# Two Strassen-Winograd x steps and the end of a feed-forward: the order of products, of column halves and of additions to x

## The chip, the cores and the metric

The kernel runs on one core of one Trainium2 chip. The core has TensorE (PE in the profile; its weight loads are PEld), VectorE (DVE), ScalarE (ACT), GpSimd (POOL, unused here but for setting up) and SyncE (SP), whose queue issues the transfers from memory. Each engine works through its own queue in order; semaphores join them. Matmul results go to PSUM, eight banks of 128 x 512 float32. The metric is the time of one launch on the device in microseconds (us).

## The reference

A two-layer encoder over 256 tokens with 2048 columns, all in float32.

```python
x = x + neighbourhood_attention(rms_norm(x, na_norm), ...)       # layer 0
x = x + sq_relu_mlp(rms_norm(x, ffn0_norm), ffn0_w1, ffn0_w2)
x = x + dilated_attention(rms_norm(x, dil_norm), ...)            # layer 1
x = x + sq_relu_mlp(rms_norm(x, ffn1_norm), ffn1_w1, ffn1_w2)
return rms_norm(x, final_norm)

def sq_relu_mlp(h, w1, w2):                                      # w1: 2048 x 8192, w2: 8192 x 2048
    return jnp.square(jax.nn.relu(h @ w1)) @ w2
```

## The kernel before

**Precision.** Every float32 operand is split into a high part rounded to the matmul's own format (wh, xT, hT: ScalarE, line 190) and the rest (wl: VectorE, line 191). A product is three matmuls: high x high, high x low, low x high (lines 195 to 197).

**Steps.** The whole kernel is one list of steps, and the loop at the end of the file runs them in turn. A step is one weight tile of 128 x 4 x 512 and has four quarters of matmuls. Around them the loop puts other work, in this order: the quarter's matmuls, the transposes and small matmuls asked for at that quarter, `after[n]` (functions that follow quarter n), `prep(i + 2, n)` (casting the weights of the step two further on), and what has to be done with the transposes. After the four quarters come `evac`, the rest of the casting (`prep(i + 2, 3)`), `load(i + 5)` (the transfers of the step five further on, on SP's queue) and `post`. So the order of each engine's queue is written out by hand.

**A feed-forward** (`ffn`) goes four times through: two gemms of w1 (each 1024 of the 2048 hidden columns of that quarter), squared relu, transposes of the result to hT, and two gemms of w2 (each 1024 columns of x, into which the result is added). 

**A gemm** (`gemm_pair`) is eight steps, one for each pair of 128-row blocks of the inner dimension. Six of them, kind "s", multiply 2 x 2 blocks in the usual way: 8 products, 24 matmuls, into the four banks "2" (rows 0, columns 0), "3" (rows 0, columns 1), "4" (rows 1, columns 0) and "S" (rows 1, columns 1). Two, kind "x" (pairs 3 and 5), use seven products of sums of blocks: 21 matmuls, and four further banks "1", "5", "6", "7". The sums on the weights' side are made by VectorE and split again: sums (line 136), hs (ScalarE, line 176), ls (line 133); part of `prep_x`. The table X gives the seven in order, two to a quarter, with the number of the weight part that each takes: 2 and 3 are cast with the step's first half, 4 to 7 are the sums, 1 is cast last.

After the last x step `begin` puts banks "1", "6", "7", "5" together into a tile C of four quarters (rows x columns), one operation behind each quarter of the step that follows. After each quarter of the gemm's last step `end` adds the bank of that quarter. For w1, squared relu then works on C. For w2, `residual` adds C to x, 1024 columns at a time, when the step is over (`rows`).

**Banks.** `sum_banks` gives a gemm its eight banks and lets two neighbours swap halves: the banks "1", "6", "7", "5" of a gemm are the "2", "4", "S", "3" of the one before. Until a gemm's first x step they are spare, in the order "1", "6", "7", "5", and transposes take them (`ps.misc`): the four transposed groups of w1's second gemm, for instance, during the second and third step of the w2 gemm that follows; VectorE's last read of such a bank is hT, line 191.

**The ends of the two feed-forwards.** At the end of a feed-forward each 512 columns of x get their squares summed (`squares`), are transposed (`transposes`, line 384) and scaled into xT (`parts`, lines 407, 410, 412). Behind the first feed-forward stands the dilated attention's first gemm (`gemm_cols`, lines 220 and 222), of kind "a". There the third and fourth 512 columns are transposed in the attention's first and second step, then 1 / rms is spread by matmuls (`rows`, line 427, `cols`, line 441). Behind the second feed-forward stands the final norm; there alone the last gemm goes by `split_end`: the last two steps finish the left 512 columns first and then the right ones, both steps' weights being read in turn.

```python
for n in range(4):
    s.quarters(s, n)
    ...
    elif i and n < 3:
        prep(i + 2, n)
    ...
for f in s.evac:
    f()
...
prep(i + 2, 3)
load(i + 5)
for f in s.post:
    f()
```

Of the kernel before, what the change touches and what calls it, by code (L numbers as in the profile page):

```python
# [14 lines left out]
P = 128  # L15
T = 256
D = 2048
# [30 lines left out]
def tile_encoder(ctx: ExitStack, tc: tile.TileContext, ins, out):  # L48
# [217 lines left out]
    def sum_banks():  # L266

        if ps.order is None:
            l = ps.pair
            a, b = (l + 1) % 3, (l + 2) % 3  # L270
            ps.order = [2 * a, 2 * a + 1, 2 * b, 2 * b + 1, 6, 7, 2 * l, 2 * l + 1]
        order, ps.order = ps.order, ps.order[4:] + ps.order[:4]
        ps.spare = order[4:]
        return {q: order[n] for n, q in enumerate(("2", "4", "S", "3", "1", "6", "7", "5"))}

    STD = {(0, 0): "2", (0, 1): "3", (1, 0): "4", (1, 1): "S"}

    def gemm_pair(w, cp, A, sums_of, order, finish, split_end=False):
# [13 lines left out]
        def product(bank, a, b, last):  # L292
            if not q:
# [4 lines left out]
        X = (("1", "A11", 2), ("2", "A12", 3), ("6", "S2", 6), ("7", "S3", 4), ("5", "S1", 5), ("4", "A22", 7),  # L298
             ("3", "S4", 1))

        for n, (kind, pair) in enumerate(order):
# [7 lines left out]
            else:  # L309
                def quarter(s, m, pair=pair, n=n):  # L310
                    tb, c = ((0, 0), (1, 0), (1, 1), (0, 1))[m]
# [21 lines left out]
        def begin(m):  # L333
            if m == 0:
                C = q["C"] = part.pool.tile([P, 4, 512], F32, name="C", tag="C")
                nc.scalar.copy(C[:, 0, :], q["1"])
                q["U"] = scratch([P, 512], "U")
                subtract(nc.vector, q["U"], q["6"], C[:, 0, :])
            elif m == 1:
                subtract(nc.vector, q["C"][:, 2, :], q["U"], q["7"])  # L340
            elif m == 2:
                add(nc.vector, q["C"][:, 1, :], q["U"], q["5"])
            else:
                add(nc.vector, q["C"][:, 3, :], q["C"][:, 2, :], q["5"])

        def end(m):
            C = q["C"]
            if m == 0:
                add(nc.vector, C[:, 0, :], C[:, 0, :], q["2"])
            elif m == 1:  # L350
                subtract(nc.vector, C[:, 2, :], q["4"], C[:, 2, :])
            elif m == 2:
                add(nc.vector, C[:, 3, :], C[:, 3, :], q["S"])
            else:
                add(nc.vector, C[:, 1, :], C[:, 1, :], q["3"])

        s = made[first_x[-1] + 1]
        for m in range(4):
            s.after[m].append(lambda m=m: begin(m))
            if not split_end:  # L360
                made[-1].after[m].append(lambda m=m: end(m))
        finish(made, q)
        return made

# [300 lines left out]
    FF_LAST = [FF_ORDER[k] for k in (0, 1, 3, 2, 5, 4, 6, 7)]  # L665
# [6 lines left out]
    def ffn(norm, w1, w2, next_norm, next_done):  # L672
        for g in range(4):
            hT, sums = [None] * 4, {}

            def hidden(made, q, cp, hT=hT, sums=sums):
# [7 lines left out]
                for m, (tb, n) in enumerate(((0, 0), (1, 0), (1, 1), (0, 1))):  # L684
# [33 lines left out]
            def residual(made, q, cp):  # L718
                if last and next_norm() in fin and cp == 1:
                    def early():  # L720
                        add(nc.vector, x[:, 0, D // 2:], x[:, 0, D // 2:], both(q, 0))
                        subtract(nc.vector, x[:, 1, D // 2:D - 512], x[:, 1, D // 2:D - 512], q["C"][:, 2, :])
                        add(nc.vector, x[:, 1, D - 512:], x[:, 1, D - 512:], q["C"][:, 3, :])
                    made[-3].evac.append(early)
                    for tb in range(2):
                        made[-2].evac.append(lambda tb=tb: add(
                            nc.vector, x[:, tb, D // 2:D - 512], x[:, tb, D // 2:D - 512], q[STD[tb, 0]]))
                    made[-2].post.append(lambda: fin[0].squares(NB - 2))
                    made[-1].after[1].append(lambda: fin[0].finish(0, q["3"]))
                    made[-1].after[3].append(lambda: fin[0].finish(1, q["S"]))  # L730
                    return

                def rows(tb):
                    to = x[:, tb, cp * 1024:(cp + 1) * 1024]
                    add(nc.vector, to, to, both(q, tb))
                made[-1].evac.append(lambda: rows(1))
                made[-1].evac.append(lambda: rows(0))
                if last:
                    for c in (2 * cp, 2 * cp + 1):
                        made[-1].post.append(lambda c=c: next_norm().squares(c))  # L740
                        if next_done is not None:
                            next_done(made[-1], c, c % 2)

            def both(q, tb):
                return q["C"][:, 2 * tb:2 * tb + 2, :].rearrange("p a n -> p (a n)")

            for cp in range(2):
                end = last and next_norm() in fin and cp == 1
                gemm_pair(w2g, cp, hT, sums, FF_LAST if end else FF_ORDER,
                          lambda made, q, cp=cp: residual(made, q, cp), split_end=end)  # L750
# [161 lines left out]
    class Final:  # L912
# [32 lines left out]
        def finish(self, tb, acc):  # L945
            cs = slice((NB - 1) * 512, D)
            nc.vector.tensor_tensor(out=x[:, tb, cs], in0=x[:, tb, cs], in1=acc, op=ALU.add)
# [66 lines left out]
    for i, s in enumerate(steps):  # L1014
# [31 lines left out]
        if i < len(steps) - 2:  # L1046
            s.w = s.hi = s.lo = s.hs = s.sums = s.pair = None
# [66 lines left out]
```

## Time and profile before

| | |
|---|---|
| median of 3 runs | 2309.98 us (2309.74 to 2311.31) |
| the profiled execution | 2308.4 us, span 2306.6 us, mean granted clock 0.998 |
| PE busy | 2273.0 us, 99% of the span |
| DVE busy | 1758.8 us, 76% |
| ACT busy | 1217.7 us, 53% |
| DMA | 430.33 MB, mean 187 GB/s |

The span runs from the first to the last instruction; the time has what lies around it too. A matmul's end is modelled, so that two in a row overlap in the rows, and "busy" for PE is not PE at its peak. A line of the timeline gives start, duration, engine, line of the kernel, what is written from what, shapes, count, and in brackets how long the engine stood idle before and who ended that. A line of the waits gives engine and line that waited, who ended the wait, then us in total, times and the longest.

### The profile page before, as it was taken

The numbers are of one execution on the slowest core, as the hardware profiler recorded it, in microseconds if no ns is written. First come the engines' busy times: TensorE is split into PE (matmuls) and PEld (weight loads), VectorE is DVE, ScalarE is ACT, GpSimd is POOL, SyncE is SP. The second block draws the span as 40 slices with busy tenths as digits, with TensorE's granted clock in tenths as the row PEclk, the third lists the DMA queues.
The fourth block names the chain that finished last, engine by engine and source line by source line (L and its number), as shares of the span: only waits on it lengthen the run. The fifth ranks groups of instructions, "written<-read, shape, count | busy, mean of one in ns | idle before, by whom it ended". The sixth has DMA issues, their size and how long they took to land.

```text
span 2306.6 us, 28352 instructions
## 1 busy us (share of the span) xinstructions
PE 2273.0 (99%) x10988; PEld 1898.0 (82%) x10988; DVE 1758.8 (76%) x2082; ACT 1217.7 (53%) x1526; POOL 0.7 (0%) x6
## 2 busy tenths in 40 slices
PE   9999999999999999999999999999999999999998
PEld 7888888888888888887788888888888888888886
DVE  6666766788788788788877667757888788788787
ACT  6444545564564564565444544456554654554554
POOL 0000000000000000000000000000000000000000
PEclk9999999999999999999999999999999999999999
DMA  7555655656656656655554555555666566566563
GB/s 250 173 175 174 193 185 167 191 181 210 186 182 206 194 177 208 200 167 180 178 198 167 184 171 181 175 172 161 184 209 187 183 205 196 182 201 201 182 219 128
DMA packets 110727, 430.33 MB, mean 187 GB/s; under 512 B 23872, under 2 KB 24448, under 8 KB 92160
## 3 DMA queue, kind: packets, MB, share of 16 engines
q1 hardware_dynamic: 109920, 426.82, 57.4%
q8 instruction: 86, 1.41, 0.2%
q10 hardware_dynamic: 672, 1.70, 0.2%
q14 instruction: 49, 0.40, 0.0%
HBM read 426.38 MB, written 2.10 MB: 186 GB/s over the span
## 4 chain that ended last, share of the span: by engine, by line
PE 87%; DVE 5%; ACT 5%; issue 2%; DMA 1%; SPq 0%; ACTq 0%; DVEq 0%
PE banks L195 22%; PE banks L196 22%; PE banks L197 22%; PE banks L220 13%; PE banks L222 6%; ACT wh L190 2%; DVE wl L191 1%; DVE sums L136 1%; DVE ls L133 1%; ACT C L681 1%; ACT hs L176 1%; PE banks L694 1%; PE banks L384 1%; ACT C L682 0%; DMA bias<-in_rpb_dram 0%
## 5 line engine op out<-in xcount | busy, mean ns | idle before, releaser
L191 DVE TENSOR_TENSOR wl<-w,wh 128x1024 fp32r<-128x1024 f32 (+1 forms) x802 | 931.5, 1176 | 389.5 <-ACT wh L190 385.7
L190 ACT CAST wh<-w 128x1024 fp32r<-128x1024 f32 (+1 forms) x802 | 804.6, 1014 | 691.6 <-PE banks L197 478.4
L220 PE MATMUL banks<-xT,wh 128*128 128x512 f32 x1280 | 455.6, 399 | 0.5 <-ACT wh L190 0.4
L195 PE MATMUL banks<-wh,xT 128*128 128x512 f32 x1152 | 453.7, 394 | 0.0
L197 PE MATMUL banks<-wh,xT 128*128 128x512 f32 x1152 | 449.3, 390 | 0.0
L196 PE MATMUL banks<-wl,xT 128*128 128x512 f32 x1152 | 448.6, 389 | 0.6 <-DVE wl L191 0.6
L222 PE MATMUL banks<-xT,wl 128*128 128x256 f32 x1280 | 358.5, 280 | 2.3 <-DVE wl L191 2.3
L195 PE MATMUL banks<-wh,hT 128*128 128x512 f32 x832 | 327.2, 393 | 0.0
L197 PE MATMUL banks<-wh,hT 128*128 128x512 f32 x832 | 324.4, 390 | 0.0
L196 PE MATMUL banks<-wl,hT 128*128 128x512 f32 x832 | 323.8, 389 | 0.0
L220 PEld LDWEIGHTS banks<-xT,wh 128*128 128x128 f32 x1280 | 241.6, 189 | 55.6 <-ACT wh L190 1.5
L197 PEld LDWEIGHTS banks<-wh,xT 128*128 128x128 f32 x1152 | 216.2, 188 | 45.8
L196 PEld LDWEIGHTS banks<-wl,xT 128*128 128x128 f32 x1152 | 216.5, 188 | 43.9 <-DVE wl L191 0.9
L195 PEld LDWEIGHTS banks<-wh,xT 128*128 128x128 f32 x1152 | 216.5, 188 | 42.7
L222 PEld LDWEIGHTS banks<-xT,wl 128*128 128x128 f32 x1280 | 242.4, 189 | 3.7 <-DVE wl L191 3.4
L176 ACT CAST hs<-sums 128x2048 fp32r<-128x2048 f32 x64 | 122.5, 1914 | 156.5 <-DVE sums L136 156.5
L197 PEld LDWEIGHTS banks<-wh,hT 128*128 128x128 f32 x832 | 156.2, 188 | 33.0
L196 PEld LDWEIGHTS banks<-wl,hT 128*128 128x128 f32 x832 | 156.4, 188 | 31.8
L195 PEld LDWEIGHTS banks<-wh,hT 128*128 128x128 f32 x832 | 156.3, 188 | 31.3
L133 DVE TENSOR_TENSOR ls<-sums,hs 128x2048 fp32r<-128x2048 f32 x64 | 146.7, 2292 | 43.6 <-ACT hs L176 43.6
L136 DVE TENSOR_TENSOR sums<-sums,w 128x512 f32<-128x512 f32 x128 | 88.6, 692 | 4.4
L136 DVE TENSOR_TENSOR C<-C,banks 128x512 f32<-128x512 f32 x125 | 82.5, 681 | 0.0
(190 smaller groups left out, 2137.7 us busy)
## 6 DMA issues: line engine op xcount, KB each, us to landing
w<-in_ffn_w_dram SPq DMA_DIRECT2D x512, 512.0 KB, 5.0
w<-in_dil_wqkv_dram SPq DMA_DIRECT2D x72, 1024.0 KB, 4.9
w<-in_na_wqkv_dram SPq DMA_DIRECT2D x47, 1024.0 KB, 5.2
w<-in_na_wo_dram SPq DMA_DIRECT2D x16, 1024.0 KB, 4.9
w<-in_dil_wo_dram SPq DMA_DIRECT2D x8, 1024.0 KB, 4.8
bias<-in_rpb_dram SPq DMA_DIRECT2D x32, 96.0 KB, 8.6
out_dram<-x SPq DMA_DIRECT2D x8, 256.0 KB, 2.5
x<-in_x_dram SPq DMA_DIRECT2D x3, 512.0 KB, 9.0
```

The lines of the kernel that those rows point to most:

```text
L133: engine.tensor_tensor(out=out, in0=a, in1=b, op=ALU.subtract)
L136: engine.tensor_tensor(out=out, in0=a, in1=b, op=ALU.add)
L176: nc.scalar.copy(s.hs, s.sums)
L190: nc.scalar.copy(dst_hi, src)
L191: nc.vector.tensor_tensor(out=dst_lo, in0=src, in1=dst_hi.bitcast(F32), op=ALU.subtract)
L195: nc.tensor.matmul(o, left[0], right[0], start=start, stop=False)
L196: nc.tensor.matmul(o, left[0], right[1], start=False, stop=False)
L197: nc.tensor.matmul(o, left[1], right[0], start=False, stop=stop)
L220: nc.tensor.matmul(o, s.hi[a][:, cs], xt.rearrange("p h t -> p (h t)"), start=first, stop=False)
L222: nc.tensor.matmul(o[:, :T], s.lo[a][:, cs], xt[:, 0, :], start=False, stop=last)
L384: nc.tensor.transpose(self.tp[:, a, tb * P:(tb + 1) * P], x[:, tb, kt * P:(kt + 1) * P], ident)
L681: nc.scalar.activation(c, c, AF.Relu, scale=norm.r[:, tb:tb + 1])
```

## The change

- In the table X, product "5" moves from fifth to last of the seven; "4" and "3" move up.
- `begin` no longer has a tile U: 6 - 1 goes straight into C's second quarter, and bank "5" is added to two quarters of C by one operation of 1024 columns that reads the bank twice. It has three parts in place of four.
- `end` goes. For w1 the last addition to C stands in `last_sum`, at the same place. For w2 C is added to x during the last step (`early`), and each finished bank is added straight to x behind its quarter (`put`), 512 columns at a time.
- The last gemm of the first feed-forward too ends by column halves (`split_end`), with pairs 3 and 4 in changed places, so that its x steps are the fifth and sixth. Its third 512 columns of x are finished a step earlier, are transposed in its last step, in banks "2" and "4", and the fourth in the attention's first step.
- The tiles of a step are let go a step later.

```diff
@@ -271,8 +271,10 @@
             ps.order = [2 * a, 2 * a + 1, 2 * b, 2 * b + 1, 6, 7, 2 * l, 2 * l + 1]
         order, ps.order = ps.order, ps.order[4:] + ps.order[:4]
         ps.spare = order[4:]
-        return {q: order[n] for n, q in enumerate(("2", "4", "S", "3", "1", "6", "7", "5"))}
-
+        ps.taken = {q: order[n] for n, q in enumerate(("2", "4", "S", "3", "1", "6", "7", "5"))}
+        return ps.taken
+
+    QUARTERS = (0, 0), (1, 0), (1, 1), (0, 1)
     STD = {(0, 0): "2", (0, 1): "3", (1, 0): "4", (1, 1): "S"}
 
     def gemm_pair(w, cp, A, sums_of, order, finish, split_end=False):
@@ -295,8 +297,8 @@
             three(q[bank], a, b, bank not in touched, last)
             touched.add(bank)
 
-        X = (("1", "A11", 2), ("2", "A12", 3), ("6", "S2", 6), ("7", "S3", 4), ("5", "S1", 5), ("4", "A22", 7),
-             ("3", "S4", 1))
+        X = (("1", "A11", 2), ("2", "A12", 3), ("6", "S2", 6), ("7", "S3", 4), ("4", "A22", 7), ("3", "S4", 1),
+             ("5", "S1", 5))
 
         for n, (kind, pair) in enumerate(order):
             k, u = pair // 2, pair % 2
@@ -308,7 +310,7 @@
                         product(bank, left(pair, a), (s.hi[b], s.lo[b]), n == first_x[-1] and bank in "1567")
             else:
                 def quarter(s, m, pair=pair, n=n):
-                    tb, c = ((0, 0), (1, 0), (1, 1), (0, 1))[m]
+                    tb, c = QUARTERS[m]
                     for kk in range(2):
                         b = 2 * (1 - c) + kk
                         a = (("A11", "A12"), ("A21", "A22"))[tb][kk]
@@ -334,33 +336,25 @@
             if m == 0:
                 C = q["C"] = part.pool.tile([P, 4, 512], F32, name="C", tag="C")
                 nc.scalar.copy(C[:, 0, :], q["1"])
-                q["U"] = scratch([P, 512], "U")
-                subtract(nc.vector, q["U"], q["6"], C[:, 0, :])
+                subtract(nc.vector, C[:, 1, :], q["6"], C[:, 0, :])
             elif m == 1:
-                subtract(nc.vector, q["C"][:, 2, :], q["U"], q["7"])
+                subtract(nc.vector, q["C"][:, 2, :], q["C"][:, 1, :], q["7"])
             elif m == 2:
-                add(nc.vector, q["C"][:, 1, :], q["U"], q["5"])
-            else:
-                add(nc.vector, q["C"][:, 3, :], q["C"][:, 2, :], q["5"])
-
-        def end(m):
-            C = q["C"]
-            if m == 0:
-                add(nc.vector, C[:, 0, :], C[:, 0, :], q["2"])
-            elif m == 1:
-                subtract(nc.vector, C[:, 2, :], q["4"], C[:, 2, :])
-            elif m == 2:
-                add(nc.vector, C[:, 3, :], C[:, 3, :], q["S"])
-            else:
-                add(nc.vector, C[:, 1, :], C[:, 1, :], q["3"])
+                add(nc.vector, q["C"][:, 1::2, :], q["C"][:, 1:3, :], q["5"].unsqueeze(1).to_broadcast([P, 2, 512]))
 
         s = made[first_x[-1] + 1]
-        for m in range(4):
-            s.after[m].append(lambda m=m: begin(m))
-            if not split_end:
-                made[-1].after[m].append(lambda m=m: end(m))
+        for m in range(3):
+            s.after[0 if s is made[-1] else m].append(lambda m=m: begin(m))
         finish(made, q)
         return made
+
+    def last_sum(q, tb, c, out):
+
+        C, own = q["C"][:, 2 * tb + c, :], q[STD[tb, c]]
+        if (tb, c) == (1, 0):
+            subtract(nc.vector, out, own, C)
+        else:
+            add(nc.vector, out, C, own)
 
 
     class Norm:
@@ -662,7 +656,6 @@
 
     FF_PAIRS = (3, 5)
     FF_ORDER = [("x" if k in FF_PAIRS else "s", k) for k in range(8)]
-    FF_LAST = [FF_ORDER[k] for k in (0, 1, 3, 2, 5, 4, 6, 7)]
 
     parts = {len(steps) + 9: "feed-forward"}
     out_rows(ins["na_wo"], na_oT, 4, lambda: norms[1], begin_norm(1, False, FF_PAIRS),
@@ -681,7 +674,8 @@
                     nc.scalar.activation(c, c, AF.Relu, scale=norm.r[:, tb:tb + 1])
                     nc.scalar.activation(c, c, AF.Square)
 
-                for m, (tb, n) in enumerate(((0, 0), (1, 0), (1, 1), (0, 1))):
+                for m, (tb, n) in enumerate(QUARTERS):
+                    made[-1].after[m].append(lambda tb=tb, n=n: last_sum(q, tb, n, q["C"][:, 2 * tb + n, :]))
                     at_after(i, m, lambda tb=tb, n=n: squared_relu(tb, n))
                 for r in range(4):
                     held = {}
@@ -715,39 +709,56 @@
             w2g = w2[4 * g:4 * (g + 1)]
             last = g == 3
 
-            def residual(made, q, cp):
-                if last and next_norm() in fin and cp == 1:
-                    def early():
-                        add(nc.vector, x[:, 0, D // 2:], x[:, 0, D // 2:], both(q, 0))
-                        subtract(nc.vector, x[:, 1, D // 2:D - 512], x[:, 1, D // 2:D - 512], q["C"][:, 2, :])
-                        add(nc.vector, x[:, 1, D - 512:], x[:, 1, D - 512:], q["C"][:, 3, :])
-                    made[-3].evac.append(early)
+            def to(cp, tb, c):
+                return x[:, tb, cp * 1024 + c * 512:cp * 1024 + (c + 1) * 512]
+
+            def residual(made, q, cp, parted):
+                def put(tb, c):
+                    add(nc.vector, to(cp, tb, c), to(cp, tb, c), q[STD[tb, c]])
+
+                def early(n):
+                    C = q["C"]
+                    if n == 0:
+                        o = x[:, 0, cp * 1024:(cp + 1) * 1024]
+                        add(nc.vector, o, o, C[:, 0:2, :].rearrange("p a n -> p (a n)"))
+                    else:
+                        subtract(nc.vector, to(cp, 1, 0), to(cp, 1, 0), C[:, 2, :])
+                        add(nc.vector, to(cp, 1, 1), to(cp, 1, 1), C[:, 3, :])
+
+                if not parted:
+                    for n in range(2):
+                        made[-1].after[n].append(lambda n=n: early(n))
+                    for m, (tb, c) in enumerate(QUARTERS):
+                        made[-1].after[m].append(lambda tb=tb, c=c: put(tb, c))
+                    if last:
+                        for c in (2 * cp, 2 * cp + 1):
+                            made[-1].post.append(lambda c=c: next_norm().squares(c))
+                            if next_done is not None:
+                                next_done(made[-1], c, c % 2)
+                    return
+                for n in range(2):
+                    made[-2 if next_done is not None else -3].evac.append(lambda n=n: early(n))
+                for tb in range(2):
+                    made[-2].after[1 + 2 * tb].append(lambda tb=tb: put(tb, 0))
+                made[-2].post.append(lambda: next_norm().squares(NB - 2))
+                if next_norm() in fin:
                     for tb in range(2):
-                        made[-2].evac.append(lambda tb=tb: add(
-                            nc.vector, x[:, tb, D // 2:D - 512], x[:, tb, D // 2:D - 512], q[STD[tb, 0]]))
-                    made[-2].post.append(lambda: fin[0].squares(NB - 2))
-                    made[-1].after[1].append(lambda: fin[0].finish(0, q["3"]))
-                    made[-1].after[3].append(lambda: fin[0].finish(1, q["S"]))
+                        made[-1].after[1 + 2 * tb].append(lambda tb=tb: fin[0].finish(tb, lambda: put(tb, 1)))
                     return
-
-                def rows(tb):
-                    to = x[:, tb, cp * 1024:(cp + 1) * 1024]
-                    add(nc.vector, to, to, both(q, tb))
-                made[-1].evac.append(lambda: rows(1))
-                made[-1].evac.append(lambda: rows(0))
-                if last:
-                    for c in (2 * cp, 2 * cp + 1):
-                        made[-1].post.append(lambda c=c: next_norm().squares(c))
-                        if next_done is not None:
-                            next_done(made[-1], c, c % 2)
-
-            def both(q, tb):
-                return q["C"][:, 2 * tb:2 * tb + 2, :].rearrange("p a n -> p (a n)")
+                for tb in range(2):
+                    made[-1].after[1 + 2 * tb].append(lambda tb=tb: put(tb, 1))
+                made[-1].post.append(lambda: next_norm().squares(NB - 1))
+                made[-2].post.append(lambda: ps.spare.extend([ps.taken["2"], ps.taken["4"]]))
+                next_done(made[-2], NB - 2)
+                next_done(made[-1], NB - 1)
 
             for cp in range(2):
-                end = last and next_norm() in fin and cp == 1
-                gemm_pair(w2g, cp, hT, sums, FF_LAST if end else FF_ORDER,
-                          lambda made, q, cp=cp: residual(made, q, cp), split_end=end)
+                parted = last and cp == 1
+                order = FF_ORDER
+                if parted:
+                    order = [FF_ORDER[k] for k in ((0, 1, 2, 4, 3, 5, 6, 7), (0, 1, 3, 2, 5, 4, 6, 7))[next_done is None]]
+                gemm_pair(w2g, cp, hT, sums, order, lambda made, q, cp=cp, parted=parted: residual(made, q, cp, parted),
+                          parted)
 
     ffn(norms[1], ins["ffn0_w1"], ins["ffn0_w2"], lambda: norms[2], begin_norm(2, True))
 
@@ -942,9 +953,8 @@
                 nc.vector.tensor_scalar(out=self.part, in0=self.part, scalar1=1.0 / D, scalar2=EPS,
                                         op0=ALU.mult, op1=ALU.add)
 
-        def finish(self, tb, acc):
-            cs = slice((NB - 1) * 512, D)
-            nc.vector.tensor_tensor(out=x[:, tb, cs], in0=x[:, tb, cs], in1=acc, op=ALU.add)
+        def finish(self, tb, put):
+            put()
             self.square(NB - 1, tb)
             ms = small.tile([P, 1], F32, name="fms", tag="fms", bufs=2)
             nc.vector.tensor_scalar(out=ms, in0=self.ss[:, tb, NB - 1:], scalar1=1.0 / D,
@@ -1043,8 +1053,9 @@
         for f in s.post:
             f()
         run_late()
-        if i < len(steps) - 2:
-            s.w = s.hi = s.lo = s.hs = s.sums = s.pair = None
+        if i:
+            p = steps[i - 1]
+            p.w = p.hi = p.lo = p.hs = p.sums = None
     part.end()
 
 
```

## The prediction

> **What bounds the kernel now.** I read the profile's page first, then TensorE's waits (us in total, times, longest), then the page's DMA issues (KB, us to landing).
>
> ```profile
> span 2306.6 us, 28352 instructions
> PE 2273.0 (99%) x10988; PEld 1898.0 (82%) x10988; DVE 1758.8 (76%) x2082; ACT 1217.7 (53%) x1526; POOL 0.7 (0%) x6
> ...
> PE banks L195 <- DVE hT L191: 6.9, 8, 0.9
> PE banks L196 <- DVE ls L133: 3.3, 3, 1.4
> PE banks L384 <- DVE x L136: 0.8, 2, 0.4
> ...
> w<-in_ffn_w_dram SPq DMA_DIRECT2D x512, 512.0 KB, 5.0
> ```
>
> TensorE is busy for 2273.0 of 2306.6 us, so only the waits can be won: at most 33.6 us, and here the largest item is one wait that comes eight times. The timeline shows it at the first of the eight (start, duration, instruction, idle before).
>
> ```profile
> 513.16 0.40 PE L196 MATMUL banks<-ls,hs 128*128 128x512 f32 x1
> 513.39 0.40 PE L197 MATMUL banks<-hs 128*128 128x512 f32 x1
> 514.66 0.50 PE L195 MATMUL banks<-hs,hT 128*128 128x512 f32 x1 [0.86 <-DVE hT L191]
> 515.00 0.40 PE L196 MATMUL banks<-ls,hT 128*128 128x512 f32 x1
> ...
> 513.92 0.68 DVE L191 TENSOR_TENSOR hT<-banks,hT 128x512 fp32r<-128x512 f32 x1
> 520.31 2.29 DVE L133 TENSOR_TENSOR ls<-sums,hs 128x2048 fp32r<-128x2048 f32 x1 [0.85 <-ACT hs L176]
> 523.94 0.40 PE L196 MATMUL banks<-ls,hs 128*128 128x512 f32 x1
> ```
>
> The waiting matmul opens the third quarter of the first x step of a w2 gemm, product "5". Its factors are old; what is new is its bank. It was the fourth spare bank, so the last of the four transposed groups of the gemm before lies in it, and VectorE reads that until 513.92 + 0.68 = 514.60. TensorE goes on 0.06 later.
>
> The other cluster lies where the first feed-forward ends; the attention's first matmul is the row 1109.35.
>
> ```profile
> 1065.00 0.66 PE L384 MATMUL banks<-ident,x 128*128 128x128 f32 x4 [0.43 <-DVE x L136]
> 1083.65 0.50 PE L196 MATMUL banks<-ls,hs 128*128 128x512 f32 x1 [1.37 <-DVE ls L133]
> 1095.10 0.50 PE L196 MATMUL banks<-ls,hs 128*128 128x512 f32 x1 [0.75 <-DVE ls L133]
> 1107.99 0.39 PE L195 MATMUL banks<-wh,hT 128*128 128x512 f32 x1
> 1108.67 0.39 PE L195 MATMUL banks<-wh,hT 128*128 128x512 f32 x1
> 1109.35 0.39 PE L220 MATMUL banks<-xT,wh 128*128 128x512 f32 x1
> 1111.81 0.40 PE L220 MATMUL banks<-xT,wh 128*128 128x512 f32 x1
> 1112.67 0.66 PE L384 MATMUL banks<-ident,x 128*128 128x128 f32 x4 [0.34 <-DVE x L136]
> 1114.57 0.60 PE L384 MATMUL banks<-ident,x 128*128 128x128 f32 x4
> 1114.92 0.48 PE L220 MATMUL banks<-xT,wh 128*128 128x512 f32 x1
> 1119.60 0.66 PE L384 MATMUL banks<-ident,x 128*128 128x128 f32 x4 [0.19 <-DVE gx L410]
> 1121.31 0.71 PE L427 MATMUL banks<-ident,rw 128*128 128x128 f32 x4 [1.05 <-DVE gx L410]
> 1125.29 0.65 PE L384 MATMUL banks<-ident,x 128*128 128x128 f32 x4 [1.86 <-DVE gx L410]
> ```
>
> Seven waits, 5.99 us by the brackets. The profile models a matmul's end 0.16 behind the next regular start (0.39 against (1108.67 - 1107.99) / 3 = 0.227), so by starts each wait is about 0.16 longer, and where a weight load was held up too (1083.65, 1095.10) up to 0.6: I count 8.1. Behind the last, the table by windows shows a stretch at half clock:
>
> ```profile
> 1119.49:1122.90 3.41, 2.25 (x14) 1.87 (x15) 3.31 (x8) 1.65 (x3) 0.00 (x0) 1.00 0.00 0
> 1122.90:1126.31 3.41, 1.55 (x11) 1.20 (x10) 3.06 (x6) 0.33 (x1) 0.00 (x0) 1.00 0.72 223
> 1126.31:1129.73 3.42, 3.42 (x12) 2.87 (x12) 2.46 (x5) 1.55 (x3) 0.00 (x0) 0.50 0.22 89
> ```
>
> (length, then busy PE, PEld, DVE, ACT, POOL, then the granted clock.) A window with PE busy for 2.25 of 3.41 was followed by full clock, one with 1.55 by 0.50, which costs 3.42 / 2 = 1.7.
>
> VectorE's and ScalarE's prices, from the same stretch:
>
> ```profile
> 1088.10 1.22 DVE L136 TENSOR_TENSOR sums<-w 128x1024 f32<-128x1024 f32 x1
> 1089.35 1.42 DVE L136 TENSOR_TENSOR sums<-sums,w 128x512 f32<-128x512 f32 x2
> 1092.75 2.29 DVE L133 TENSOR_TENSOR ls<-sums,hs 128x2048 fp32r<-128x2048 f32 x1 [0.84 <-ACT hs L176]
> 1109.06 1.28 DVE L136 TENSOR_TENSOR C<-C,banks 128x512 f32<-128x512 f32 x2
> 1110.26 2.35 DVE L136 TENSOR_TENSOR x<-x,C 128x1024 f32<-128x1024 f32 x2
> 1118.21 0.48 DVE L410 TENSOR_SCALAR gx<-banks,gT 128x256 f32<-128x256 f32 x1
> 1119.07 0.48 DVE L410 TENSOR_SCALAR gx<-banks,gT 128x256 f32<-128x256 f32 x1
> 1109.55 1.05 ACT L190 CAST wh<-w 128x1024 fp32r<-128x1024 f32 x1 [1.66 <-PE banks L197]
> ```
>
> In a queue an instruction starts 0.08 or 0.09 before the end shown of the one in front: a 512 addition takes 0.60 of VectorE's time (1110.26 - 1109.06, halved), a 1024 one 1.13, ls 2.2, a gx/xT pair 0.86 (1119.07 - 1118.21).
>
> **Part 1, product "5" last.** Two products (six matmuls) go ahead of it. The x step's pitch is 0.23 (513.39 - 513.16), so without a wait it opens at 513.39 + 7 x 0.234 = 515.02, 0.36 after the bank is free. The wait goes whole. From 513.39 to 515.00 lie 1.61 for two pitches of 0.234: each instance costs 1.14, eight cost 9.1. What is late next: ls of the second x step of that gemm ends at 520.31 + 2.29 = 522.60, by VectorE's own queue. TensorE will want it at 523.94 - 1.14 = 522.80 in place of 523.94: 0.15 to spare after the 0.05 of signalling. Product "3" is now sixth. That x step starts seven pitches before the ls matmul, so now at 521.2, and "3" at 521.2 + 15 x 0.234 = 524.7; its piece, the 512 subtraction behind ls, is there at 520.31 + 2.2 + 0.7 = 523.2. Both hold, the first just. **-9.1.**
>
> **Part 2, sums without U.** U goes; C1 takes its place at the same 0.68. Two 512 additions from a bank become one of 1024 that reads the bank twice. No row shows that form. It lies between 1.22 (sums<-w, also one operand read twice, from SBUF) and the 1.28 of the pair it replaces; I take 1.22. Thirty-two times less than 0.1 on VectorE, while TensorE runs the step after the last x step and waits for nothing in the list: 0. Were the cover gone, a few us at most.
>
> **Part 3, x in quarters.** In a w2 gemm VectorE did 4 x 0.60 + 2 x 1.13 = 4.7, the last 2.3 behind the step's end; now 1.13 + 6 x 0.60 = 4.7, nearly all inside it. The same work. No PE wait stands between these gemms (the list's x waits are the two rows 1065.00 and 1112.67), so it is worth 0 but for 1065.00: the columns transposed there are ready 2.3 of queue earlier. That wait goes.
>
> **Part 4, the first feed-forward's end.** Here I laid the three queues in program order, each instruction at the later of its engine's turn and its input, at the intervals above. For the kernel before this puts the seven waits within 0.2 of their rows. For the new order:
>
> The x steps move to positions 4 and 5. The loads of the two steps that change places change places on SP's queue too; both have 512 KB twice, are issued some three steps (16 us) before they are cast and land 5.0 after issue, so nothing waits for them; POOL issues nothing here. The wait of 1083.65 goes, since VectorE has a plain step in between. Two x steps follow each other: from ls to ls VectorE needs 1.25 + 0.72 + 0.60 (sums) + 1.13 (wl) + 0.93 (the 0.84 for hs, by starts) + 2.2 + 0.6 = 7.4, TensorE 21 x 0.234 = 4.9; the first ls has 1.25 to spare, so the second makes TensorE wait **1.3**.
>
> Let T be the start of position 6 (a quarter is 6 x 0.227 = 1.36). Its quarters read the right-hand half-buffers of both last steps in turn, so the buffer for the attention's first weights is free only after the third quarter: wh at T + 4.08 + 0.2, wl from T + 5.37. Behind wl on VectorE stand the merged addition, put(1,0), early(0) and the first half of early(1): T + 5.37 + 1.13 + 1.13 + 0.60 + 1.13 + 0.69 = T + 10.05. For those TensorE's moved transposes wait, due at T + 8.16: **1.9**. It then needs 0.35 + 1.36 + 0.35 + 1.36 to the attention and 8 x 0.351 to the transposes of the last columns: due T + 16.4. VectorE: wl, put(0,1), wl (its wh again a quarter late, T + 13.1), four gx/xT pairs 3.4, put(1,1): T + 18.4. **2.0.** Then transposes, row and column matmuls find their banks free: the waits of 1119.60 to 1125.29 go, as the columns before were moved up a step.
>
> So 8.1 become 5.3, and four restarts fewer at 0.11 (0.34 in place of 0.23 behind the row 514.66) make 0.4: **-3.2**. Which buffer wh gets I can bound: the first one freed (the 1.36 above; the tiles tagged "o" only fit four buffers if buffers go by release), or strict turns, where wh for the attention's second half waits till T + 9.5 and the last wait grows from 2.0 to 4.2. I take the first.
>
> **The clock.** Both new waits of about 2 leave PE some 1.6 busy in a window that holds one wholly, near the 1.55 that was followed by 0.50. I keep one half-clock window: 0. [...]
>
> **Part 5, the second feed-forward's end.** Its early sums and order stand; put(0,0) moves up a step's half, but VectorE's queue and then TensorE's end decide there as before: 0.
>
> **Sum.** -9.1 - 3.2 = -12.3 against the profiled execution's 2308.4 (span 2306.6 and 1.8 around it): 2296.1. The runs' median 2309.98 is 1.6 above; from it 2297.7.
>
> **Rivals.** (a) No half-clock window is left: a further 1.7, 2296.0. For it: one window with 2.25 busy kept the clock; against: 1.6 is nearer 1.55. [...] (b) Strict turns of the weight buffers: part 4 wins 0.6 + 0.4 at most; 2309.98 - 9.1 - 1.0 = 2299.9. (c) VectorE's lag shows again at the next ls: the 0.15 to spare is gone if its queue slips; a slip of 1.1 gives 8 x 1.0 back: 2305.7. Against it: that queue is fed by ScalarE and loads, not by the wait removed. (d) The wait is for hT as data, not for the bank, and follows product "5" or returns elsewhere: only part 4 is left, 2306.8. Against: the factors of "5" belong to a pair that was transposed a gemm earlier. (e) Slower: product "3" is pulled 0.70 ahead in all 64 x steps, and its 512 piece is cast last of all. Were it late each time, 64 x 0.70 = 45 come in: 2342; it decides from 0.2 per step. Against: 1.5 to spare at 524.7.
>
> **How the numbers follow.** Forecast 0.52; (a) 0.24, (b) 0.10, (c) 0.06, (d) 0.05, (e) 0.03. The range reaches from (a) with the new waits of part 4 half as long (2296.0 - 2.6 = 2293.4) to beyond (b), 2302; what lies outside is (c) to (e). 0.2% is 4.6 us, about what a measurement here can tell from no change: faster is all under 2305.4, 0.91; (d) and the worst of (c) are the same, 0.06; slower 0.03.
>
> **What would show it.** TensorE's waits must no longer name hT; product "5" starts about 0.36 after the hT read of its bank. ls of the next x step must stay unnamed in w2's first gemms. Around 1050 to 1120, seven waits turn into three: one ls, two for x. A second long wait over 3, ended by x behind wl, means (b); a granted clock of 1.00 throughout means (a). I am wrong at the root if hT is still named.

## The result, and the profile after

The changed kernel takes 2296.32 us (median of four runs, 2295.2 to 2296.8) beside 2310.22 for the kernel before on the same chip (four runs). The ratio is 0.9938, 95% interval 0.9921 to 0.9956: 13.9 us less, and by the interval between 10 and 18. On another chip, five runs gave 2296.75 beside 2309.01, ratio 0.9948 (0.9936 to 0.9961), 12.3 us less. The profiled execution took 2296.8 against 2308.4.

First the head of the changed kernel's page, and from the list of waits those of TensorE for VectorE that lie at the change (us in total, times, longest; gx is what the transposed columns of x become on their way to xT).

```profile
span 2295.0 us, 28363 instructions
PE 2269.6 (99%) x10988; PEld 1898.5 (83%) x10988; DVE 1758.1 (77%) x2065; ACT 1217.3 (53%) x1526; POOL 0.7 (0%) x6
```

```profile
PE banks L196 <- DVE ls L133: 2.1, 2, 1.2
PE banks L378 <- DVE x L136: 1.9, 2, 1.2
...
PE banks L378 <- DVE gx L404: 0.7, 1, 0.7
...
PE banks L378 <- DVE x L133: 0.3, 1, 0.3
```

The item that came eight times for hT is gone from the list. VectorE is busy as long as before (1758.1 us against 1758.8) with 17 instructions fewer. The timeline shows the first of the eight places (start, duration, instruction, idle before):

```profile
515.25 0.40 PE L195 MATMUL banks<-hs,hT 128*128 128x512 f32 x1
...
515.96 0.40 PE L195 MATMUL banks<-wh,hs 128*128 128x512 f32 x1
...
516.65 0.40 PE L195 MATMUL banks<-hs,hT 128*128 128x512 f32 x1
...
524.44 0.39 PE L196 MATMUL banks<-ls,hs 128*128 128x512 f32 x1
...
515.54 0.68 DVE L191 TENSOR_TENSOR hT<-banks,hT 128x512 fp32r<-128x512 f32 x1
...
521.92 2.29 DVE L133 TENSOR_TENSOR ls<-sums,hs 128x2048 fp32r<-128x2048 f32 x1 [0.84 <-ACT hs L176]
```

Products "4" (515.25) and "3" (515.96) now run while VectorE reads the bank until 515.54 + 0.68 = 516.22. Product "5" opens at 516.65, 0.43 later, without a wait. At the next x step ls is ready at 524.21 and taken at 524.44.

The end of the first feed-forward, in the same timeline:

```profile
1090.36 0.51 PE L196 MATMUL banks<-ls,hs 128*128 128x512 f32 x1 [1.16 <-DVE ls L133]
...
1103.31 0.33 PE L378 MATMUL banks<-ident,x 128*128 128x128 f32 x1 [1.19 <-DVE x L136]
1103.90 0.55 PE L378 MATMUL banks<-ident,x 128*128 128x128 f32 x3 [0.27 <-DVE x L133]
...
1111.21 0.33 PE L378 MATMUL banks<-ident,x 128*128 128x128 f32 x1 [0.73 <-DVE gx L404]
1112.27 0.55 PE L378 MATMUL banks<-ident,x 128*128 128x128 f32 x3 [0.73 <-DVE x L136]
...
1099.16 1.23 DVE L191 TENSOR_TENSOR wl<-w,wh 128x1024 fp32r<-128x1024 f32 x1 [1.68 <-ACT wh L190]
1100.30 1.22 DVE L136 TENSOR_TENSOR C<-C,banks 128x1024 f32<-128x1024 f32 x1
...
1103.16 0.69 DVE L133 TENSOR_TENSOR x<-x,C 128x512 f32<-128x512 f32 x1
...
1111.54 0.68 DVE L136 TENSOR_TENSOR x<-x,banks 128x512 f32<-128x512 f32 x1
...
1098.07 1.05 ACT L190 CAST wh<-w 128x1024 fp32r<-128x1024 f32 x1 [3.29 <-PE banks L197]
1099.43 1.06 ACT L190 CAST wh<-w 128x1024 fp32r<-128x1024 f32 x1 [0.30 <-PE banks L197]
```

Seven waits have become three clusters. Counted from matmul start to matmul start, less the regular pitch (0.23 at 512 columns, 0.11 at 256), they are 1.33 (ls), 1.36 + 0.54 (x) and 0.90 + 1.00 (bank, then x): 5.1 in all. The same count, called "by starts" from here on, gives 7.2 for the kernel before. And the granted clock, from the table by windows (length, then busy PE, PEld, DVE, ACT, POOL, then the clock):

```profile
1099.68:1103.09 3.41, 2.43 (x11) 1.69 (x9) 3.41 (x4) 0.81 (x1) 0.00 (x0) 1.00 0.17 70
...
1109.92:1113.33 3.41, 1.95 (x12) 1.35 (x11) 3.34 (x7) 1.45 (x4) 0.00 (x0) 1.00 0.00 0
1113.33:1116.74 3.41, 3.41 (x23) 3.04 (x22) 2.88 (x11) 2.79 (x7) 0.00 (x0) 1.00 0.72 216
```

No stretch at half clock is left behind these waits: the clock is 1.00 from 11 us to 2287 us of the span.

Every kernel here issues the same number of matmuls, 10988, so two traces can also be compared between matmuls of the same number. From number 1800 (339 us, behind the first attention) to the last, the changed kernel is 13.2 us faster than the kernel before: 8.9 at the eight places, 4.1 between numbers 4952 and 5700 (1043 to 1193 us, the end of the first feed-forward), 0.2 at the end of the second.

### The profile page after: what moved, and what is told of

It is laid out like the page before. It is cut to its first block, busy times and chain, and to the rows that moved or that the text cites. A ratio compares the mean times of both kernels' runs of the same rounds, so it can differ in the third digit from the quotient of the medians.

```text
span 2295.0 us, 28363 instructions
## 1 busy us (share of the span) xinstructions
PE 2269.6 (99%) x10988; PEld 1898.5 (83%) x10988; DVE 1758.1 (77%) x2065; ACT 1217.3 (53%) x1526; POOL 0.7 (0%) x6
## 4 chain that ended last, share of the span: by engine, by line
PE 94%; DVE 3%; ACT 1%; DMA 1%; issue 1%; SPq 0%; ACTq 0%; DVEq 0%
PE banks L196 24%; PE banks L197 24%; PE banks L195 24%; PE banks L220 13%; PE banks L222 7%; PE banks L688 1%; DMA bias<-in_rpb_dram 1%; DVE wl L191 1%; PE banks L378 1%; ACT wh L190 1%; DVE x L136 0%; DVE sums L136 0%; PE banks L880 0%; PE banks L840 0%; PE banks L591 0%
## 5 line engine op out<-in xcount | busy, mean ns | idle before, releaser
L136 DVE TENSOR_TENSOR sums<-w 128x1024 f32<-128x1024 f32 x64 | 78.0, 1219 | 0.0
```

The lines of the kernel that those rows point to most:

```text
L136: engine.tensor_tensor(out=out, in0=a, in1=b, op=ALU.add)
```

## The experiments

Each was timed beside the kernel before on its chip: 2308.81 us for the first four runs, 2309.01 for the next four, 2309.71 for the last.

**1. The order of the products alone.** The kernel before, with only the new table X.

```diff
-        X = (("1", "A11", 2), ("2", "A12", 3), ("6", "S2", 6), ("7", "S3", 4), ("5", "S1", 5), ("4", "A22", 7),
-             ("3", "S4", 1))
+        X = (("1", "A11", 2), ("2", "A12", 3), ("6", "S2", 6), ("7", "S3", 4), ("4", "A22", 7), ("3", "S4", 1),
+             ("5", "S1", 5))
```

> The kernel before with product 5 moved to the end of the seven, nothing else. Bank theory: TensorE's eight waits for hT go and each instance gives back 1.14 us, so 9.1 us less than before, about 2301.1 us; the waits at the first feed-forward's end stay as they were, with their half-clock window. Rival theory, that the gain of 13.9 us comes from VectorE's lighter queue (sums without U, x in quarters) and the order only shifts a wait: within 2 us of before, above 2308 us, with a wait named behind the move (ls of the next x step, 0.15 us to spare).

Measured: 2299.51, ratio 0.9959 (0.9947 to 0.9972), 9.3 less. hT is gone from the waits; between matmuls of the same number TensorE gains 1.11 to 1.14 at each of the eight places, and the seven other waits stand (7.1 by starts). Part 1 of the sum holds. One thing did not come as expected: this profile has no stretch at half clock, which gives it another 1.5 between numbers 4952 and 5700.

**2. The change without it.** The changed kernel with the old table X.

> The changed kernel with product 5 back in fifth place. Bank theory: hT is named eight times again with 1.04 us by starts, so 9.1 us more than the changed kernel, about 2305.4 us. Rival theory (VectorE's lighter queue carries the gain): less than 3 us more than the changed kernel, 2296 to 2299 us, and no wait or a short one for hT.

Measured: 2305.8 (eleven runs), ratio 0.9985 (0.9976 to 0.9994), 3.0 less than before. The waits of this kernel have the old row again:

```profile
PE banks L195 <- DVE hT L191: 6.9, 8, 0.9
```

9.3 and 3.0 make 12.3: by the medians the order of the products and the rest add up. By matmul number this kernel gains 4.1 between 4952 and 5700, as the changed kernel does (about 1.5 of it because here too no stretch at half clock is left), and elsewhere from 1800 on it stays within 0.2 of the kernel before. So the rest of the change (sums, quarters, halves, tiles let go later) acts at the end of the first feed-forward alone.

**3. The change without the column halves.** The changed kernel, but the first feed-forward's last gemm is not parted and keeps its order.

```diff
-                parted = last and cp == 1
+                parted = last and cp == 1 and next_done is None
```

> The changed kernel, but the last gemm of the first feed-forward in the old order of steps and not by column halves; x is still added to in quarters. Laying out the queues, the waits around the end are two for ls (1.9 together), one for bank and norm (0.9), one for a bank (2.1): 5.0 us where the changed kernel has 5.3, so by waits alone the column halves are worth nothing, and 2296.3 to 2298.0 us with a half-clock window behind the last wait or without. Rival theory, that the column halves carry the 3.2 us of part 4 as the prediction's text gives it to them: 2299.5 us or more.

Measured: 2296.92, ratio 0.9946 (0.9934 to 0.9959), 11.9 less than before: the same as the whole change within the intervals. So the 3.0 of the second run don't need the halves. The waits left there are two of 0.9 and 0.8 for ls and two for gx, 0.9 and 2.0, together 4.7. Its timeline and windows show the half clock, this time behind that wait of 2.0:

```profile
1118.65 0.66 PE L378 MATMUL banks<-ident,x 128*128 128x128 f32 x4 [1.86 <-DVE gx L404]
```

```profile
1116.11:1119.52 3.41, 1.55 (x11) 1.14 (x10) 3.21 (x7) 0.17 (x1) 0.00 (x0) 1.00 0.70 207
1119.52:1122.94 3.42, 3.42 (x13) 2.94 (x12) 2.18 (x5) 1.71 (x3) 0.00 (x0) 0.50 0.26 105
```

**4. The last transposed group in another bank.** The kernel before, with the spare banks in another order: the last group lies in bank "1", which the x step's first product takes. If the wait follows the bank, it moves to the start of the x step; if it follows hT as data, it stays.

```diff
-        ps.spare = order[4:]
+        ps.spare = [order[7], order[5], order[6], order[4]]
```

> The kernel before with banks 1 and 5 exchanged among the spare ones, so that the last transposed group lies in bank 1, which the x step's first product writes; the matmuls and their data are the same. Bank theory: TensorE now waits at the start of that x step until VectorE has read the bank, about 3.8 us in place of 1.04, eight times: 22 us more than before, 2332 us, and up to 1.7 us more for each wait that brings a half-clock window, 2346 us at most. Rival theory, that product 5 waits for hT as data: no change, 2310 us, and the wait stays at the third quarter.

Measured: 2349.63, ratio 1.0175 (1.0159 to 1.019), 40.8 more than before. From its waits and its timeline, at two of the eight places:

```profile
PE banks L195 <- DVE hT L191: 28.9, 8, 3.6
...
PE banks L195 <- DVE gx L410: 4.3, 1, 4.3
```

```profile
516.98 0.50 PE L195 MATMUL banks<-wh,hT 128*128 128x512 f32 x1 [3.61 <-DVE hT L191]
...
1731.15 0.50 PE L195 MATMUL banks<-wh,hT 128*128 128x512 f32 x1 [3.61 <-DVE hT L191]
```

The wait now stands at the x step's first matmul: it belongs to the bank. By starts it is 3.8 in place of 1.03, eight times 2.8 more, 22. At the end of the first feed-forward a wait of 4.5 for gx comes in and two for ls go, 2.4 together. Some 16 are left, and the profile has nine stretches at half clock ahead of the final norm, 48 us long in all, where the kernel before has one of 3.4 (mean granted clock 0.989 against 0.998). Seven of the eight places have one behind them; by matmul number they lose 1.4 to 2.8 more than the eighth, where the clock stays, 14.6 together. The time is above the 2346 that the expectation gave as the most: it had no wait for gx, and it priced a stretch at the 3.4 us of the kernel before, while some last twice as long. The windows around the two rows above:

```profile
514.24:517.66 3.42, 0.68 (x3) 0.59 (x4) 3.34 (x5) 2.26 (x3) 0.00 (x0) 1.00 0.61 156
517.66:521.07 3.41, 3.41 (x10) 2.62 (x9) 3.34 (x5) 1.44 (x2) 0.00 (x0) 0.50 0.93 282
...
1725.98:1729.39 3.41, 1.56 (x8) 0.96 (x6) 3.18 (x8) 3.21 (x6) 0.00 (x0) 1.00 0.00 0
1729.39:1732.80 3.41, 1.65 (x7) 1.38 (x8) 3.41 (x4) 1.28 (x2) 0.00 (x0) 1.00 0.87 271
```

The same wait of 3.61 was followed by half clock at the first place, where the row that holds most of it has PE busy for 0.68, and at the second, where it lies half in each of two rows (1.56 and 1.65), both rows have 1.00.

**5. VectorE's additions earlier.** The rows 1099.16 to 1103.16 above show why TensorE waits for x: behind wl, which itself waits for the late buffer of wh, stand the merged addition, one quarter of x and both early additions. This kernel has the sums of C behind the first quarter of the step before the last, and the early additions behind its second, all ahead of wl; the transposes come a quarter later.

```diff
-            s.after[0 if s is made[-1] else m].append(lambda m=m: begin(m))
+            s.after[0 if s in made[-2:] else m].append(lambda m=m: begin(m))
...
-                    made[-2 if next_done is not None else -3].evac.append(lambda n=n: early(n))
+                    (made[-3].evac if next_done is None else made[-2].after[1]).append(lambda n=n: early(n))
...
-                made[-2].post.append(lambda: ps.spare.extend([ps.taken["2"], ps.taken["4"]]))
-                next_done(made[-2], NB - 2)
+                made[-2].post.append(lambda: ps.spare.extend([ps.taken["4"], ps.taken["2"]]))
+                next_done(made[-2], NB - 2, first=2)
```

> The changed kernel with VectorE's work in the last two steps of the first feed-forward put otherwise: the three sums of C all behind the first quarter of the step before the last, both early additions behind its second quarter instead of behind the whole step, and the third columns of x transposed at the last step's third and fourth quarter instead of second and third, bank 4 before bank 2. Theory (the two waits for x, 1.90 and 1.90 us, exist because VectorE reaches the additions behind two casts of weights): both waits go, 3.8 less than the changed kernel, ratio to before about 0.9925, and no wait for x above 0.4 in the profile. Rival (VectorE is simply late by its sum of work there, and whoever reads it next waits instead): the waits move to gx or to the attention's weights and the time stays within 1.0 of the changed kernel.

Measured: 2292.41 (2292.25 to 2294.03), ratio 0.9931 (0.9919 to 0.9944), 4.3 under the changed kernel timed beside it (run 6). Its timeline:

```profile
1102.70 0.60 PE L378 MATMUL banks<-ident,x 128*128 128x128 f32 x4
...
1107.78 0.60 PE L378 MATMUL banks<-ident,x 128*128 128x128 f32 x4
...
1114.77 0.60 PE L421 MATMUL banks<-ident,rw 128*128 128x128 f32 x3 [0.31 <-DVE gx L404]
...
1096.37 1.22 DVE L136 TENSOR_TENSOR C<-C,banks 128x1024 f32<-128x1024 f32 x1
...
1099.37 0.69 DVE L136 TENSOR_TENSOR x<-x,C 128x512 f32<-128x512 f32 x1
...
1100.57 1.22 DVE L191 TENSOR_TENSOR wl<-w,wh 128x1024 fp32r<-128x1024 f32 x1
1101.71 0.68 DVE L136 TENSOR_TENSOR x<-x,banks 128x512 f32<-128x512 f32 x1
...
1106.97 0.68 DVE L136 TENSOR_TENSOR x<-x,banks 128x512 f32<-128x512 f32 x1
```

Both waits for x are gone (1102.70 and 1107.78 have no bracket); half a microsecond comes back at 1114.77, by starts 0.48. By matmul number this kernel is 3.0 faster than run 6 between 4952 and 5700 and 3.1 from 1800 to the last, so about 1 of the 4.3 is not in these two traces. The order of VectorE's queue made the waits, not its sum of work (busy 1758.2 us here, 1758.1 in run 6). Which edit took them away, the earlier additions or the later transposes, this run doesn't show. The last addition to the columns of the first wait ends at 1102.39: with the transposes a quarter (1.36) earlier, at their old place, about 1.1 of the wait would be left, and with the later place alone about 0.5 of the 1.90; both are estimates from these rows and those of run 6. The addition that ends the second wait is done at 1107.65 in place of 1111.52 (run 6); it stands behind two pairs of gx and xT in place of four, and these moved with the transposes. This is the fastest of all the kernels here.

**6. The changed kernel again**, beside run 5.

> The changed kernel itself on this chip, for comparing the others with it. Forecast of the same sum as before: 12.3 less than the kernel before, ratio 0.9947; with one half-clock window fewer 14.0 less, 0.9939.

Measured: 2296.75 (2295.52 to 2298.2), ratio 0.9948: 12.3 less than before.

**7. The halves without the quarters.** The changed kernel, but in the gemms that do not end by halves x is added to in whole rows behind the step, as before.

```diff
-                    for n in range(2):
-                        made[-1].after[n].append(lambda n=n: early(n))
...
-                        made[-1].after[m].append(lambda tb=tb, c=c: put(tb, c))
+                        made[-1].after[m].append(lambda tb=tb, c=c: last_sum(q, tb, c, q["C"][:, 2 * tb + c, :]))
+                    for tb in (1, 0):
+                        made[-1].evac.append(lambda tb=tb: add(
+                            nc.vector, x[:, tb, cp * 1024:(cp + 1) * 1024], x[:, tb, cp * 1024:(cp + 1) * 1024],
+                            q["C"][:, 2 * tb:2 * tb + 2, :].rearrange("p a n -> p (a n)")))
```

> The changed kernel, but x is again added to in whole rows of 1024 columns behind the step in every gemm except the one that ends the first feed-forward by halves and the last of all (those go by halves and quarters as in the change). Theory A (halves and quarters each take away the same lateness of VectorE, so one of them alone is nearly enough): only the wait of 0.6 at the start of that last gemm comes back, 0.6 more than the changed kernel. Theory B (all of the 2.6 beyond the new order of products comes from the quarters in the gemm before, which lets VectorE enter the last gemm 2.3 earlier): 2.4 more than the changed kernel, about 9.5 less than before, ratio 0.9959. By the forecast's own account of the parts: 0.6 more.

Measured: 2297.86, ratio 0.9953 (0.994 to 0.9967), 1.1 over the changed kernel: nearer theory A, though times this close lie within each other's intervals. By matmul number it loses 1.3 against the changed kernel between 4952 and 5700, more than theory A's 0.6 and less than B's 2.4. The trace shows the two parts: the old wait at the start of that gemm is back (0.60 by starts), and ls costs 1.65 in place of 1.33.

```profile
1060.19 0.66 PE L378 MATMUL banks<-ident,x 128*128 128x128 f32 x4 [0.43 <-DVE x L136]
1089.55 0.50 PE L196 MATMUL banks<-ls,hs 128*128 128x512 f32 x1 [1.47 <-DVE ls L133]
```

**8. The same at the second feed-forward's end.** Run 5, and the last gemm of all gets the same order of steps and the same places of its additions.

```diff
-                    order = [FF_ORDER[k] for k in ((0, 1, 2, 4, 3, 5, 6, 7), (0, 1, 3, 2, 5, 4, 6, 7))[next_done is None]]
+                    order = [FF_ORDER[k] for k in (0, 1, 2, 4, 3, 5, 6, 7)]
...
-                    (made[-3].evac if next_done is None else made[-2].after[1]).append(lambda n=n: early(n))
+                    made[-2].after[1].append(lambda n=n: early(n))
```

> As the run with early sums, and the second feed-forward's last gemm gets the same order of steps (x steps fifth and sixth) and the same places of the sums and early additions. Theory: the wait for ls there (1.12 us in the changed kernel) goes, since a plain step lies between, and nothing at the end is later, because the last columns are added only behind the last step's quarters: 1.1 less than with early sums alone. Rival: two x steps in succession bring a wait for ls of 1.3 there as they did at the end of the first feed-forward, and the additions come later in front of the final norm: 0.2 to 2 more than with early sums alone.

Measured: 2293.69, ratio 0.9934 (0.9922 to 0.9947): no gain over run 5. The wait of 1.1 for ls is gone, yet what follows the last matmul takes as much back. Run 5, then this one (TensorE ran 1.5 later here than in run 5 before matmul 1800, so that the same time of the last matmul is a gain of 1.4):

```profile
2280.39 0.39 PE L197 MATMUL banks<-wh,hT 128*128 128x512 f32 x1
...
2281.83 0.68 DVE L136 TENSOR_TENSOR x<-x,banks 128x512 f32<-128x512 f32 x1
```

```profile
2280.43 0.39 PE L197 MATMUL banks<-wh,hT 128*128 128x512 f32 x1
...
2283.29 0.68 DVE L136 TENSOR_TENSOR x<-x,banks 128x512 f32<-128x512 f32 x1
```

VectorE's last addition comes 2.86 behind the last matmul's start in place of 1.44: the second part of the rival, 1.4 in size, as much as was won. Its first part, a wait of 1.3 for ls, did not come.

**9. The sums with U.** The changed kernel with `begin` in four parts as before.

> The changed kernel with the sums of C made as before: 6 - 1 goes into a tile U, bank 5 is added by two operations of 512 in two quarters of the step, four parts in place of three. The forecast's part 2: same time as the changed kernel, since TensorE runs the step behind the last x step without a wait (ratio to before 0.9947). Rival: at the end of the first feed-forward, where VectorE is behind, the pair of additions takes 1.28 in place of 1.22 and its second half comes a quarter later, so the wait for x of 1.90 grows by what the second half is later than the merged addition, up to 0.7.

Measured: 2295.74, ratio 0.994 (0.9926 to 0.9953), the same as the changed kernel. At the one place where VectorE is late, the pair ends at about the time of the merged addition, and the wait for x is 1.42 by starts in place of 1.36:

```profile
1102.45 0.33 PE L381 MATMUL banks<-ident,x 128*128 128x128 f32 x1 [1.25 <-DVE x L136]
```

## Why the prediction was right, and where not

The forecast of 2297.7 stands 1.4 and 0.9 above the two medians, and 12.3 is what runs 1 and 2 add up to and what run 6 gives. Two of its steps were nevertheless wrong, and their errors partly cancelled: part 4 was put 0.6 too high, and the clock, put at 0, gave 1.5. That the total came out so close is in part luck. Rival (a), at 2296.0, lies even nearer to the medians of 2296.32 and 2296.75; with intervals of 3 to 4 us to either side the times can't tell the two apart, but the profiles show what (a) says.

**Part 1** held: -9.1 forecast, 9.3 measured alone, 8.9 by matmul number at the eight places; product "5" 0.43 behind its bank where 0.36 was forecast; ls with 524.44 - 524.21 = 0.23 to spare, 0.15 to 0.20 forecast. Rival (d) fell with runs 1 and 4, (c) and (e) with the missing waits in w2's gemms.

**Part 2** held: 0 (run 9), and the merged addition took 1.22, the value that was taken for a form that no row had shown.

**Part 3 failed as put.** "It is worth 0 but for 1065.00" overlooked that VectorE, freed 2.3 earlier, is also earlier at the next gemm's first ls and at its end. Run 3 against run 1 has the merged sums, the quarters and the tiles let go later as its edits beyond the order, and is 2.6 faster; run 9 gives the sums nothing, and no run takes the later release alone. In run 3 the first ls wait falls from 1.53 to 0.90, the one of 0.6 goes, and three of 0.51, 0.36 and 1.27 become one of 0.94.

**Part 4: the queue layout was right, its price was not.** The layout gave 1.3, 1.9 and 2.0; the profile has 1.33, 1.90 and 1.90. The buffers go to the first release, as taken: wh at 1098.07 and 1099.43, one quarter apart, so rival (b) fell. But "I count 8.1" for the waits before was too much: by starts they are 7.2, and the addition of up to 0.6 for a held-up weight load was not there (1.53 and 0.91 by starts beside 1.37 and 0.75 in brackets). Of the 4.1 gained there by matmul number about 1.5 are the stretch at half clock (run 1, whose waits there stand, gains 1.5). That leaves 2.6, which is the 7.2 - 5.1 = 2.1 and some restarts, not 3.2. The 5.3 put for the new waits is also 0.1 more than its three terms.

And the halves get no credit that the quarters don't have too. Between numbers 4952 and 5700, without what the clock gives, the halves alone gain 1.3 (run 7), the quarters alone 2.7 (run 3), both together 2.6. The medians say the same less sharply: 1.8, 2.6 and 3.0 beyond run 1, where each time has an interval of about 3 us to either side. Each takes away the same lateness of VectorE.

**The clock step failed.** "Both new waits of about 2 leave PE some 1.6 busy in a window that holds one wholly": the second lies wholly in a window, and PE is 1.95 busy there, since the wait comes in two pieces, with the modelled end of a matmul at each. The row behind it has a clock of 1.00, so "I keep one half-clock window" was wrong; rival (a) came to pass in both profiled executions (the first and run 6), worth about 1.5. In the first profile TensorE also runs 1.7 later from the first attention on, which no part of the change touches, and that took as much back: its last matmul is 11.6 earlier.

## What to carry to other kernels

A wait that names a tensor may be a wait for its bank or buffer: look at what last read the place the instruction writes, and put work that writes elsewhere in between; reordering the products was worth about three quarters of this change (9.3 of 12.3). When an engine's lateness causes several waits, several edits can each remove it and their gains do not add (1.3 and 2.7 alone, 2.6 together); test one without the other before crediting either. Where additions stand behind a cast that waits for a buffer, moving them ahead of it can win the wait (run 5, 3.0 to 4.3 us together with transposes put a quarter later), unless a later part of the same queue sets the end (run 8, where 1.4 came back there).

## What the runs showed that was not expected

The granted clock did not go by the length of a wait alone: behind one of 1.86 it was 0.50 in run 3, behind one of 3.61 it was 0.50 at 516.98 in run 4 and stayed at 1.00 at 1731.15. Of the rows of 3.41 us at full clock, those followed by 0.50 have PE busy for 1.55 (the kernel before and run 3) and for 0.68 (run 4); those followed by 1.00 have 1.56 (at 1725.98 in run 4), 1.95 (the changed kernel), 2.25 (the kernel before) and 2.04 (run 1). What decides the clock the runs don't show. Behind the same wait of about 1.9 for gx it was 0.50 in the kernel before and stayed at 1.00 in run 1:

```profile
1117.99:1121.41 3.42, 2.04 (x12) 1.59 (x12) 3.38 (x6) 0.00 (x0) 0.00 (x0) 1.00 0.28 55
1121.41:1124.82 3.41, 2.91 (x18) 2.58 (x19) 2.51 (x7) 1.75 (x3) 0.00 (x0) 1.00 0.62 257
```

By matmul number that was worth 1.5 between 4952 and 5700, with the waits there alike (7.2 and 7.1 by starts): so much of a difference between two executions can be the clock's alone.
